# One long convolution's taps on TensorE, and an output projection that begins with the other half

## The chip, the cores and the metric

The kernel runs as one program on one core of a Trainium2 chip. The metric is the device time of one execution in microseconds (us). The core has five engines with a queue each, which run in order and wait for each other by semaphores: TensorE (PE, with its weight loads as PEld), VectorE (DVE), ScalarE (ACT), GpSimd (POOL) and SyncE (SP, which here only starts transfers).

## The reference

It is one step of a two-layer model on 128 context and 512 latent tokens (640 columns here), all in float32. Layer 0 mixes tokens by two convolutions, layer 1 by attention; each is followed by a SwiGLU feed-forward block (FFN). The change touches layer 0's mixer only:

```
u = h @ w_in
ya = gate_b * depthwise_conv(gate_c * xa, sc_w)            # short: 3 taps, 512 channels
z = ub[..., :512] * sigmoid(ub[..., 512:])
z = depthwise_conv(z, cf_dw_w) + cf_dw_b                   # long: 31 taps, 512 channels
z = silu(layernorm(z, cf_ln_g, cf_ln_b))                   # over the 512 channels
return concatenate([ya, z], axis=-1) @ w_out + b_out
```

Context and latent tokens are convolved as separate sequences. What follows needs the mixer's whole output row: an RMS norm, the residual sum, a second RMS norm, and then the FFN.

## The kernel before

Activations lie with channels on the 128 partitions and tokens in the free dimension. A long-convolution channel block is a tile `z0` to `z3`, a short one a tile `m0` to `m3`. Tokens are worked in two chunks: GA, columns 0 to 255, and GB, columns 256 to 639. A dense product is made from three reduced products (`mm3`, lines 175, 187 and 189: high by high, high weight by low input, low weight by high input); the weight's high part is an ACT cast (`whi`, line 134), its low part a subtraction on DVE or POOL (`wlo`, line 139). PE passes of these products are named by their output: `ub`, `gc`, `xa`, `gb` for the input projection, `po` for the output projection, `pg` and `pu` for the first FFN products.

`conv` computes the long convolutions' input first (`ub`), and then, while PE computes `gc`, `xa` and `gb`, DVE runs the 31 taps of each z tile as multiply-adds (line 798): tiles 0 and 1 over all tokens at once (`acl`, 670 columns with pads), tiles 2 and 3 in two groups, the first enough for GA, the second for GB (`acd`). `conv_norm` is the layer norm of one chunk: column sums on PE (`lnm`, `lnv`), the mean and the reciprocal root spread back to all partitions by PE (`spread`), the rest on DVE and ACT. `conv_out` splits the normed z into high and low, and for each chunk multiplies z and m by `w_out`: 64 mm3 steps of 3 passes for GA, and 64 for GB. `boundary` turns a chunk's output into the FFN's input `h` (two sums of squares `st`, two `spread`s, and work on DVE, ACT and POOL); GA's runs while PE does GB's output projection, GB's while PE does the FFN's first products for GA.

The order of instructions on each engine is fixed when the program is built. The taps and the norms are generators in the list `fine`; every mm3 step of a projection advances them by a tick (`lin`), at the low priority TAP_PRIO, and a scheduler then places every instruction in its engine's queue by priority and by its own idea of when inputs are ready. TAP_STEPS = 2 lets two DVE taps go per tick; TAP_ORDER is the order of tiles and groups.

Of the kernel before, what the change touches and what calls it, by code (L numbers as in the profile page):

```python
# [12 lines left out]
AF = mybir.ActivationFunctionType  # L13
ALU = mybir.AluOpType
# [3 lines left out]
P = 128  # L18
D = 1024
KD = D // P  # L20
SEQ = 128
LAT = 512
# [6 lines left out]
CFK = 31  # L29
# [8 lines left out]
AB = ((0, 256), (256, 384))  # L38
# [12 lines left out]
TAP_PRIO = -500  # L51
TAP_STEPS = 2

TAP_ORDER = ((0, None), (1, None), (2, 0), (3, 0), (2, 1), (3, 1))
XCOPY = ('dve',) * 8
SQ_DVE = (1,) * 8
ADD_DVE = (3, 6)
# [17 lines left out]
class Net:  # L75
# [688 lines left out]
    def conv(self, H, M, ada):  # L764
# [20 lines left out]
        def taps(src, wcol, K, pad, bias, out, per, group=None):  # L785
# [21 lines left out]
            c = max(a, st)  # L807
            tap(t, out[:, SEQ + c - st:SEQ + b - st], src[:, t + c:t + b], acc[:, c - a:n])

        zs = [self.ty(f"z{j}") for j in range(4)]  # L810
        made, normed = set(), set()
        for z in zs:
            zero_pads(z, 15)
        self.mix("dve")
# [2 lines left out]
        for hb, chs in ((0, GA), (0, GB), (1, AB)):  # L817
            b2 = self.block(w, 0, KD, 3 * SCW + 512 + 256 * hb, 256)
            b1 = self.block(w, 0, KD, 3 * SCW + 256 * hb, 256)
            sgs = []  # L820
            for i in range(2):
                j = 2 * hb + i
                p2 = self.lin(b2, i * P, P, H, chs, "ub2")
                sgs.append(self.t5([P, TOK], name="sgm"))
                for c, (s, n) in enumerate(chs):
                    nc.scalar.activation(sgs[i][:, s:s + n], p2[c][:, :n], AF.Sigmoid, bias=cb[:, 4 + j:5 + j])
            for i in range(2):
                j = 2 * hb + i
                z = zs[j]
                p1 = self.lin(b1, i * P, P, H, chs, "ub1")  # L830
                sg = sgs[i]
                for c, (s, n) in enumerate(chs):
                    dst, src, g = padded(z, 15, p1[c][:, :n], sg[:, s:s + n], s)
                    nc.vector.scalar_tensor_tensor(dst, src, cb[:, j:j + 1], g, ALU.add, ALU.mult)
                if chs != GA:
                    made.add(j)
            if hb == 0 and chs == GB:
                long = lambda j, per, g: taps(zs[j], lambda t: cw[:, 4 * t + j:4 * t + j + 1], CFK, 15,
                                              par["conv_cf_dw_b"][:, j:j + 1], zs[j], per, g)
                def stream(*todo):  # L840
                    todo = list(todo)
                    while todo:
                        at = next((i for i, (j, _) in enumerate(todo) if j in made), None)
                        if at is None:
                            yield
                            continue
                        j, g = todo.pop(at)
                        yield from long(j, 1, g)
                        for x in ((0, 1) if g is None else (g,)):
                            seen[x] += 1  # L850
                            if seen[x] == 4:
                                yield from self.conv_norm(zs, (GA, GB)[x])
                                normed.add(x)
                seen = [0, 0]
                self.fine.append(self.rate(stream(*TAP_ORDER), TAP_STEPS))
        scw = par["conv_sc_w"]
        for hb in range(2):
            bc = self.block(w, 0, KD, SCW + 256 * hb, 256)
# [20 lines left out]
            for i in range(2):  # L879
# [5 lines left out]
                m = self.t5([P, 2, TOK], R32, name=f"m{j}")  # L885
                self.split((m[:, 0], m[:, 1]), ya[:, :TOK])
                M.append(m)
        while 0 not in normed:
            with self.tc.high_priority(TAP_PRIO):
                self.tick(self.fine)  # L890
        return zs

    def conv_norm(self, zc, ch):

# [35 lines left out]
    def conv_out(self, w, M, Z, zs, Y, bias, after, between):  # L930

        nc = self.nc
        self.mix("pool", "dve")
        gens = []
        for ch in (GA, GB):
            if ch == GB:
                for g in self.fine + self.bg:
# [5 lines left out]
            Yg = Y(ch)  # L943
            for cb in range(4):
                wt = self.block(w, 4, 4, cb * 256, 256) + self.block(w, 0, 4, cb * 256, 256)
                for i in range(2):
                    o = 2 * cb + i
                    ps = self.lin(wt, i * P, P, Z + M, ch, "po")
                    nc.scalar.activation(Yg[o], ps[0][:, :n], AF.Identity, bias=bias[:, o:o + 1])
            gens.append(self.spawn_b(after(Yg, ch)))  # L950
        self.finish(gens[0])
        return gens[1]
# [527 lines left out]
    def run(self):  # L1480
# [13 lines left out]
        zs = self.conv(H, M, self.ada_whole(0, range(4, 10)))  # L1494
        Z = [self.t5([P, 2, TOK], R32, name=f"z{j}") for j in range(4)]
        box = {}

# [9 lines left out]

        def rows(ch):

            (s, n), = ch  # L1510
            if ch == GA:
                first = self.t5([P, 4, n], name="yoa")
                box["rest"] = [self.ty(f"yo{k}") for k in range(4, KD)]
                return [first[:, k] for k in range(4)] + [t[:, s:s + n] for t in box["rest"]]
            return [self.ty(f"yo{k}")[:, s:s + n] for k in range(4)] + [t[:, s:s + n] for t in box["rest"]]

        late = self.conv_out(I["conv_w_out"][0], M, Z, zs, rows, self.par["conv_b_out"], after, between)
        box2 = {}
        ada1 = self.ada_steps(((0, 10, 2), (1, 0, 4), (1, 4, 6)))

# [109 lines left out]
```

## Time and profile before

| | before |
|---|---|
| time of 3 runs, us | median 1736.71 (1735.44 to 1738.82) |
| the profiled execution | 1737.27 us, its span 1735.5 us |
| PE busy | 1635.7 us, 94% of the span |
| DVE busy | 1115.9 us, 64% |
| ACT busy | 669.3 us, 39% |
| chain that ended last | PE 76%, DVE 17% of the span |

Times inside the profile are microseconds from the span's start. Matmuls overlap, so what a pass costs is read from one start to the next, not from its duration (a 256-column pass lasts 0.28 and the next starts 0.12 later). An F32 product is shown as two passes. In a merged line "x2" is the count of passes, and the bracket at a line's end is the idle time ahead of it and what ended it. The mixer's last `po` pass ends, and the FFN's first product starts, at 341.20.

### The profile page before, as it was taken

The page shows a single profiled execution, that of the slowest core. Times are in us where ns is not written, and L with a number is a line of the kernel's source. Part 1 is how long each engine was busy: PE and PEld are TensorE (multiplying, and loading weights), DVE is VectorE, ACT ScalarE, POOL GpSimd, SP SyncE. Part 2 cuts the span into 40 slices and gives each one's busy share as a digit, 9 for nine tenths or more (in the row PEclk, how much of TensorE's full clock was granted, in tenths as well). Part 3 has the DMA queues.
Part 4 walks back from the last instruction along what each step waited for, and adds up shares of the span by engine and source line. Part 5 has one row for each costly group of instructions (what it writes and reads, how often), then busy time and mean ns, then how long its engine had stood idle before and what let it go on. Part 6 is the DMA issues. An engine that isn't in the chain of part 4 may idle for free.

```text
span 1735.5 us, 26938 instructions
## 1 busy us (share of the span) xinstructions
PE 1635.7 (94%) x10549; PEld 1533.4 (88%) x10549; DVE 1115.9 (64%) x2134; ACT 669.3 (39%) x1287; POOL 394.0 (23%) x319
## 2 busy tenths in 40 slices
PE   7999967989999999999898899989998999999998
PEld 3587767989999999999787798779998999999998
DVE  6389997789774725987989755775999102111236
ACT  4321125543232212235444576774642222212234
POOL 1000012443000000002534221124433243333323
PEclk9999988989999999999989999999999999999999
DMA  9543423246463423555433000025355232222233
GB/s 344 160 126 116 129 71 113 77 134 199 154 194 110 150 82 115 183 160 169 126 107 78 13 25 25 1 66 174 107 170 164 61 98 73 73 74 73 73 100 108
DMA packets 183408, 198.65 MB, mean 114 GB/s; under 512 B 21651, under 2 KB 155744, under 8 KB 183280
## 3 DMA queue, kind: packets, MB, share of 16 engines
q1 hardware_dynamic: 181232, 195.34, 36.3%
q8 instruction: 83, 1.36, 0.3%
q10 hardware_dynamic: 1600, 1.48, 0.3%
q14 instruction: 45, 0.37, 0.1%
q0 software_dynamic: 448, 0.11, 0.0%
HBM read 191.37 MB, written 5.52 MB: 113 GB/s over the span
## 4 chain that ended last, share of the span: by engine, by line
PE 76%; DVE 17%; issue 3%; ACT 2%; DMA 1%; POOL 0%; SPq 0%; DVEq 0%; ACTq 0%; POOLq 0%
PE pd L175 5%; PE pd L187 5%; PE pd L189 5%; PE pu L175 5%; PE pu L187 5%; PE pu L189 5%; PE pg L187 5%; PE pg L189 5%; PE pg L175 5%; PE av L1417 3%; PE adaw L491 3%; DVE sq L548 2%; PE pT L973 2%; PE po L175 2%; PE po L189 2%
## 5 line engine op out<-in xcount | busy, mean ns | idle before, releaser
L134 ACT CAST whi<-raw 128x1024 fp32r<-128x1024 f32 (+1 forms) x260 | 263.2, 1017 | 439.2 <-PE pd L187 112.3
L139 POOL TENSOR_TENSOR wlo<-raw,whi 128x1024 fp32r<-128x1024 f32 (+3 forms) x120 | 284.1, 2371 | 555.0 <-ACT whi L134 520.1
L139 DVE TENSOR_TENSOR wlo<-raw,whi 128x1024 fp32r<-128x1024 f32 (+3 forms) x148 | 186.1, 1258 | 107.3 <-ACT whi L134 106.6
L655 DVE TENSOR_TENSOR sg<-pu,sg 128x320 f32<-128x320 f32 (+2 forms) x88 | 39.9, 483 | 247.5 <-PE pu L189 247.5
L189 PE MATMUL pd<-hid,wlo 128*128 128x320 f32 (+2 forms) x704 | 181.5, 310 | 0.0
L175 PE MATMUL pd<-hid,whi 128*128 128x320 f32 (+2 forms) x704 | 181.5, 310 | 0.0
L187 PE MATMUL pd<-hid,whi 128*128 128x320 f32 (+2 forms) x704 | 181.4, 309 | 0.0
L175 PE MATMUL pg<-h,whi 128*128 128x320 f32 (+2 forms) x704 | 177.3, 312 | 3.3 <-DVE sg L655 3.3
L175 PE MATMUL pu<-h,whi 128*128 128x320 f32 (+2 forms) x704 | 178.8, 313 | 0.0
L187 PE MATMUL pu<-h,whi 128*128 128x320 f32 (+2 forms) x704 | 178.4, 313 | 0.0
L189 PE MATMUL pu<-h,wlo 128*128 128x320 f32 (+2 forms) x704 | 178.0, 312 | 0.0
L187 PE MATMUL pg<-h,whi 128*128 128x320 f32 (+2 forms) x704 | 177.8, 312 | 0.0
L189 PE MATMUL pg<-h,wlo 128*128 128x320 f32 (+2 forms) x704 | 177.2, 311 | 0.0
L386 DVE SCALAR_TENSOR_TENSOR acc<-adaw,cT,acc 128x512 f32<-128x512 f32 x196 | 159.4, 865 | 5.6 <-DMA adaw<-in_ada_w 4.9
L175 PEld LDWEIGHTS pg<-h,whi 128*128 128x128 f32 x704 | 123.2, 190 | 3.6 <-DVE sg L655 3.6
L175 PEld LDWEIGHTS pu<-h,whi 128*128 128x128 f32 x704 | 124.6, 192 | 0.0
L187 PEld LDWEIGHTS pu<-h,whi 128*128 128x128 f32 x704 | 124.6, 192 | 0.0
L189 PEld LDWEIGHTS pu<-h,wlo 128*128 128x128 f32 x704 | 124.5, 192 | 0.0
L187 PEld LDWEIGHTS pg<-h,whi 128*128 128x128 f32 x704 | 123.3, 190 | 0.4 <-DVE h L540 0.2
L189 PEld LDWEIGHTS pd<-hid,wlo 128*128 128x128 f32 x704 | 123.6, 189 | 0.0
L187 PEld LDWEIGHTS pd<-hid,whi 128*128 128x128 f32 x704 | 123.5, 189 | 0.0
L175 PEld LDWEIGHTS pd<-hid,whi 128*128 128x128 f32 x704 | 123.5, 189 | 0.0
(473 smaller groups left out, 3354.8 us busy)
## 6 DMA issues: line engine op xcount, KB each, us to landing
adaw<-in_ada_w SPq DMA_DIRECT2D x112, 256.0 KB, 3.0
raw<-in_ffn_w_gate SPq DMA_DIRECT2D x56, 512.0 KB, 3.7
raw<-in_ffn_w_up SPq DMA_DIRECT2D x56, 512.0 KB, 3.7
raw<-in_ffn_w_down SPq DMA_DIRECT2D x56, 512.0 KB, 3.5
raw<-in_conv_w_in SPq DMA_DIRECT2D x24, 512.0 KB, 4.5
raw<-in_ada_w SPq DMA_DIRECT2D x24, 512.0 KB, 4.2
ada0w<-in_ada_w SPq DMA_DIRECT2D x16, 512.0 KB, 10.7
raw<-in_conv_w_out SPq DMA_DIRECT2D x16, 512.0 KB, 3.6
```

The source lines that it names most:

```text
L134: nc.scalar.copy(hi[:, :kt, :cols], rv)
L139: (self.nc.vector if (le or next(self.lo_mix)) == "dve" else self.nc.gpsimd).tensor_tensor(o, x, h, ALU.subtract)
L175: ins = [mm(o, whi, h, start=first, stop=False) for o, (h, l) in zip(outs, xs)]
L187: mm(o, whi, l, start=False, stop=False)
L189: mm(o, wlo, h, start=False, stop=last)
L386: ins = nc.vector.scalar_tensor_tensor(acc[v], w, self.cT[:, v, k:k + 1], acc[v], ALU.mult, ALU.add)
L491: nc.tensor.matmul(ps[:2, :], self.cM[:, k0 + k], w[:, k], start=(k0 + k == 0), stop=(k0 + k == KD - 1))
L548: src = (nc.vector if SQ_DVE[k] else nc.gpsimd).tensor_tensor(q, q, acc, ALU.add)
L655: nc.vector.tensor_tensor(tv(sg[i]), uv, tv(sg[i]), ALU.mult)
L973: self.nc.tensor.transpose(ps, src, self.ident[:m, :m])
L1417: nc.tensor.matmul(av[:, :u.w], value(h, k), pt_[:, 0, i] if u.qt == 0 else pt_[:, :, i], start=(i == 0 and q_ == 0), stop=(i == len(ks) - ...
```

## The change

Tile 1's taps leave DVE. For each of the 31 taps ACT scales the identity matrix by that tap's column of coefficients (`dg`, a 128x128 diagonal in F32), and PE multiplies the shifted z tile by it in F32, once over GA's 256 columns and once over GB's 384, summing all taps in two PSUM tiles (`tap`). Two ACT passes add the bias and write z1 back. Every chunk's layer norm now waits for tile 1 (`tapped`). The generator gives a tap every third tick (TAP_PE_STEPS = 3).

The output projection starts with the m half for GA (all 8 output blocks) and for GB's blocks 4 to 7; ACT writes these sums with the bias. Only then the program waits for GA's norm. Then comes the z half for GA, added by DVE to what lies there; for GB, blocks 0 to 3 are made as before from z and m together, and blocks 4 to 7 from z alone, added by DVE. The PE passes of the projection are as many as before; the weight blocks it loads are 14 instead of 16.

```diff
-TAP_ORDER = ((0, None), (1, None), (2, 0), (3, 0), (2, 1), (3, 1))
+TAP_ORDER = ((0, None), (2, 0), (3, 0), (2, 1), (3, 1))
+TAP_PE = 1
+TAP_PE_STEPS = 3
...
+        def matrix_taps(j):
+            st = SEQ + 30
+            while j not in made:
+                yield
+            ps = [self.sp("tap")[:, :n] for _, n in AB]
+            ps[0] = ps[0].rearrange("p (s n) -> p s n", s=2)
+            for t in range(CFK):
+                d = t2("dg", P, 4)
+                nc.scalar.mul(d, self.ident, cw[:, 4 * t + j:4 * t + j + 1])
+                for o, x in zip(ps, (zs[j][:, t:t + 2 * st].rearrange("p (s n) -> p s n", s=2)[:, :, :SEQ],
+                                     zs[j][:, t + st + SEQ:t + st + LAT])):
+                    nc.tensor.matmul(o, d, x, start=(t == 0), stop=(t == CFK - 1))
+                yield
+            for o, (s, n) in zip(ps, AB):
+                x = zs[j][:, s:s + n]
+                nc.scalar.activation(x.rearrange("p (s n) -> p s n", s=2) if s == 0 else x, o, AF.Identity,
+                                     bias=par["conv_cf_dw_b"][:, j:j + 1])
+            tapped.add(j)
...
-                            if seen[x] == 4:
+                            if seen[x] == 3:
+                                while TAP_PE not in tapped:
+                                    yield
                                 yield from self.conv_norm(zs, (GA, GB)[x])
...
-                self.fine.append(self.rate(stream(*TAP_ORDER), TAP_STEPS))
+                self.fine += [self.rate(stream(*TAP_ORDER), TAP_STEPS), self.rate(matrix_taps(TAP_PE), 1 / TAP_PE_STEPS)]
...
+        def half(cb, k0, X, ch, outs, add):
+            wt = self.block(w, k0, 4, cb * 256, 256)
+            if len(X) > 4:
+                wt += self.block(w, 0, 4, cb * 256, 256)
+            for i in range(2):
+                o = 2 * cb + i
+                ps = self.lin(wt, i * P, P, X, ch, "po")
+                for p, (_, n), y in zip(ps, ch, outs):
+                    if add:
+                        nc.vector.tensor_tensor(y[o], p[:, :n], y[o], ALU.add)
+                    else:
+                        nc.scalar.activation(y[o], p[:, :n], AF.Identity, bias=bias[:, o:o + 1])
+        for cb in range(4):
+            half(cb, 0, M, AB if cb > 1 else GA, [Yg, rest], False)
+        while 0 not in normed:
+            with self.tc.high_priority(TAP_PRIO):
+                self.tick(self.fine)
...
             for cb in range(4):
-                wt = self.block(w, 4, 4, cb * 256, 256) + self.block(w, 0, 4, cb * 256, 256)
-                for i in range(2):
-                    o = 2 * cb + i
-                    ps = self.lin(wt, i * P, P, Z + M, ch, "po")
-                    nc.scalar.activation(Yg[o], ps[0][:, :n], AF.Identity, bias=bias[:, o:o + 1])
+                if ch == GB and cb < 2:
+                    half(cb, 4, Z + M, ch, [Yg], False)
+                else:
+                    half(cb, 4, Z, ch, [Yg], True)
```

In the built order PE meets the 31 taps late: 19 of them before the last `gb` pass, 8 among the `po` passes of the m half, and 4 behind all of these. The 62 products stand in 48 groups between other passes. The first place is PE's queue from the end of the input projection to GA's norm. Before, the norm's sums follow the last `gb` pass at once, and the whole output projection follows the norm:

```order
L187 MATMUL gb<-h_410,whi 128x256
L187 MATMUL gb<-h_410,whi 128x384
L189 MATMUL gb<-h_410,wlo 128x256
L189 MATMUL gb<-h_410,wlo 128x384
L306 MATMUL lnm<-con,lna 128x1 x2
L313 MATMUL spread<-con,mun 128x128 x2
L306 MATMUL lnv<-con,lnq 128x1 x2
L313 MATMUL spread<-con,rzn 128x128 x2
L306 MATMUL lnm<-con,lna 128x1 x3
L313 MATMUL spread<-con,mun 128x128 x3
L175 MATMUL po<-z_2234,whi 128x256 x4
```

Now (from the last pass of the m half on; `m_2326` is m3):

```order
L192 MATMUL po<-m_2326,wlo 128x384
L825 MATMUL tap<-z_498,dg 128x256
L825 MATMUL tap<-z_498,dg 128x384
L825 MATMUL tap<-z_498,dg 128x256
L825 MATMUL tap<-z_498,dg 128x384
L825 MATMUL tap<-z_498,dg 128x256
L825 MATMUL tap<-z_498,dg 128x384
L825 MATMUL tap<-z_498,dg 128x256
L825 MATMUL tap<-z_498,dg 128x384
L309 MATMUL lnm<-con,lna 128x1 x2
L316 MATMUL spread<-con,mun 128x128 x2
L309 MATMUL lnv<-con,lnq 128x1 x2
```

The m half stands ahead of the last taps, and between the last tap and GA's z half PE has only the norm's own small products. The second place is DVE's queue in GA's norm. Before, the ops of the reciprocal root stand between taps of tiles 2 and 3 for GB:

```order
L291 TENSOR_TENSOR rtn<-rgn 128x2
L798 SCALAR_TENSOR_TENSOR acd<-z_499,pcols_168,acd 128x384
L798 SCALAR_TENSOR_TENSOR acd<-z_500,pcols_168,acd 128x384
L292 TENSOR_TENSOR rtn<-rtn,rhn 128x2
L798 SCALAR_TENSOR_TENSOR acd<-z_499,pcols_168,acd 128x384
L798 SCALAR_TENSOR_TENSOR acd<-z_500,pcols_168,acd 128x384
L294 SCALAR_TENSOR_TENSOR rzn<-rtn,rgn 128x2
L798 SCALAR_TENSOR_TENSOR z_499<-z_499,pcols_168,acd 128x384
```

Now:

```order
L288 TENSOR_SCALAR rgn<-rvn 128x2
L291 TENSOR_SCALAR rhn<-rvn 128x2
L294 TENSOR_TENSOR rtn<-rgn 128x2
L295 TENSOR_TENSOR rtn<-rtn,rhn 128x2
L297 SCALAR_TENSOR_TENSOR rzn<-rtn,rgn 128x2
L294 TENSOR_TENSOR rtn<-rzn 128x2
L295 TENSOR_TENSOR rtn<-rtn,rhn 128x2
```

All taps on DVE stand far ahead of the norm. The third place is PE's queue at the end of the output projection, where GA's `h` becomes ready (`h_2518` and `h_2685` are its first tile). Before, 47 `po` passes stand between the last `spread` of GA's boundary and the FFN:

```order
L189 MATMUL po<-m_2171,wlo 128x384
L175 MATMUL po<-m_2231,whi 128x384
L187 MATMUL po<-m_2231,whi 128x384
L189 MATMUL po<-m_2231,wlo 128x384
L175 MATMUL po<-z_2234,whi 128x384
L313 MATMUL spread<-con,rzb 128x128 x2
L187 MATMUL po<-z_2234,whi 128x384
L189 MATMUL po<-z_2234,wlo 128x384
```

Now none do:

```order
L178 MATMUL po<-z_2332,whi 128x384
L190 MATMUL po<-z_2332,whi 128x384
L192 MATMUL po<-z_2332,wlo 128x384
L316 MATMUL spread<-con,rzb 128x128 x2
L178 MATMUL pg<-h_2685,whi 128x256 x2
L554 MATMUL st<-con,sq 128x1 x3
L178 MATMUL pu<-h_2685,whi 128x256
```

GB's output projection is 144 passes instead of 192 and all of them stand ahead of that `spread`. From the FFN's first blocks on, the order on every engine is the same as before.

## Rows read from the trace of the kernel before

**Rows 1.** Stretches: span; PE, PEld, DVE, ACT, POOL busy; PE clock; DMA.

```profile
80.00:243.00 163.00, 163.00 (x924) 129.87 (x923) 140.54 (x232) 29.80 (x40) 4.27 (x8) 1.00 0.39 120
243.00:273.00 30.00, 7.87 (x39) 7.38 (x38) 27.83 (x66) 7.54 (x15) 1.21 (x2) 0.56 0.19 62
273.00:300.00 27.00, 24.64 (x203) 24.45 (x202) 17.80 (x36) 18.17 (x32) 9.59 (x4) 0.98 0.38 118
300.00:343.00 43.00, 40.73 (x224) 40.13 (x225) 34.76 (x95) 25.86 (x54) 13.94 (x10) 0.92 0.32 99
343.00:381.00 38.00, 31.24 (x224) 30.80 (x223) 30.45 (x57) 14.69 (x25) 21.79 (x11) 0.87 0.36 111
```

**Rows 2.** Timeline of PE, end of input projection to output projection: start, length.

```profile
243.63 0.46 PE L189 MATMUL gb<-h,wlo 128*128 128x256 f32 x2
243.93 0.50 PE L306 MATMUL lnm<-con,lna 128*128 128x1 f32 x4
248.16 1.22 PE L313 MATMUL spread<-con,mun 128*128 128x128 f32 x4 [3.73 <-DVE mun L907]
257.68 0.99 PE L306 MATMUL lnv<-con,lnq 128*128 128x1 f32 x4 [8.30 <-DVE lnq L918]
268.26 1.19 PE L313 MATMUL spread<-con,rzn 128*128 128x128 f32 x4 [9.59 <-DVE rzn L294]
...
272.33 0.56 PE L175 MATMUL po<-z,whi 128*128 128x256 f32 x1
```

**Rows 3.** Tile acl: the taps of tiles 0 and 1 on DVE.

```profile
L798 DVE SCALAR_TENSOR_TENSOR acl<-z,pcols,acl x58: 905/916/921, 93.2 to 210.4; 128x670 f32<-128x670 f32 x58
```

**Rows 4.** Timeline of PE, F32 products among reduced ones.

```profile
221.02 0.38 PE L175 MATMUL xa<-h,whi 128*128 128x256 f32 x1
221.34 1.02 PE L491 MATMUL adaw<-raw,cM 128*2 128x512 f32 x2
222.29 0.44 PE L175 MATMUL xa<-h,whi 128*128 128x384 f32 x1
...
986.09 2.33 PE L1417 MATMUL av<-ptw,Vg 128*128 128x256 f32 x10
...
988.39 0.31 PE L1351 MATMUL s<-kL,qS 128*128 128x320 f32 x1
```

**Rows 5.** Timeline of DVE, ops of the layer norms.

```profile
251.48 1.41 DVE L912 TENSOR_TENSOR z<-spread,z 128x256 f32<-128x256 f32 x4
...
288.29 0.15 DVE L285 TENSOR_SCALAR rgn<-rvn 128x3 int32<-128x3 int32 x1
...
290.54 0.16 DVE L294 SCALAR_TENSOR_TENSOR rzn<-rtn,rzn 128x3 f32<-128x3 f32 x1
```

**Rows 6.** Timeline of PE, GA's last output pass to GB's boundary.

```profile
296.58 0.28 PE L187 MATMUL po<-m,whi 128*128 128x256 f32 x1
296.70 0.28 PE L189 MATMUL po<-m,wlo 128*128 128x256 f32 x1
...
301.24 0.94 PE L551 MATMUL st<-con,sq 128*128 128x1 f32 x4 [0.29 <-DVE sq L548]
...
309.98 0.61 PE L313 MATMUL spread<-con,rzb 128*128 128x128 f32 x4
...
310.60 0.34 PE L189 MATMUL po<-m,wlo 128*128 128x384 f32 x1
...
332.48 0.71 PE L313 MATMUL spread<-con,rzb 128*128 128x128 f32 x4 [1.64 <-DVE rzb L294]
...
341.20 0.40 PE L175 MATMUL pg<-h,whi 128*128 128x256 f32 x2
...
351.62 0.94 PE L313 MATMUL spread<-con,rzb 128*128 128x128 f32 x6 [3.36 <-DVE rzb L294]
...
370.02 1.41 PE L551 MATMUL st<-con,sq 128*128 128x1 f32 x6 [3.40 <-DVE sq L548]
```

**Rows 7.** Timeline of DVE, low parts of the second half of GA's h.

```profile
341.16 2.19 DVE L540 SCALAR_TENSOR_TENSOR h<-yo,mods,h 128x128 fp32r<-128x128 f32 x8
```

More of the change, by code (lines that the diff above doesn't have):

```diff
@@ L808, in taps @@
             tap(t, out[:, SEQ + c - st:SEQ + b - st], src[:, t + c:t + b], acc[:, c - a:n])
+        def matrix_taps(j):
[16 more added lines that the diff above has]
+            tapped.add(j)
         zs = [self.ty(f"z{j}") for j in range(4)]
-        made, normed = set(), set()
+        made, normed, tapped = set(), set(), set()
         for z in zs:
@@ L887, in conv @@
                 M.append(m)
[L888 to L891, printed above, removed]
+        return zs, normed
     def conv_norm(self, zc, ch):
@@ L928, in conv_norm, with conv_out @@
                                  bias=par["conv_cf_ln_b"][:, j:j + 1])
-    def conv_out(self, w, M, Z, zs, Y, bias, after, between):
+    def conv_out(self, w, M, Z, zs, normed, Y, bias, after, between):
         nc = self.nc
@@ L934, in conv_out @@
         gens = []
+        Yg = Y(GA)
+        rest = Y(None)
+        def half(cb, k0, X, ch, outs, add):
[15 more added lines that the diff above has]
+                self.tick(self.fine)
         for ch in (GA, GB):
@@ L942, in conv_out @@
                 self.split((Z[j][:, 0, s:s + n], Z[j][:, 1, s:s + n]), zs[j][:, s:s + n])
-            Yg = Y(ch)
+            if ch == GB:
+                Yg = Y(GB)
             for cb in range(4):
-                wt = self.block(w, 4, 4, cb * 256, 256) + self.block(w, 0, 4, cb * 256, 256)
-                for i in range(2):
-                    o = 2 * cb + i
-                    ps = self.lin(wt, i * P, P, Z + M, ch, "po")
-                    nc.scalar.activation(Yg[o], ps[0][:, :n], AF.Identity, bias=bias[:, o:o + 1])
+                if ch == GB and cb < 2:
+                    half(cb, 4, Z + M, ch, [Yg], False)
+                else:
+                    half(cb, 4, Z, ch, [Yg], True)
             gens.append(self.spawn_b(after(Yg, ch)))
@@ L1493, in run @@
         M = []
-        zs = self.conv(H, M, self.ada_whole(0, range(4, 10)))
+        zs, normed = self.conv(H, M, self.ada_whole(0, range(4, 10)))
         Z = [self.t5([P, 2, TOK], R32, name=f"z{j}") for j in range(4)]
@@ L1508, in rows @@
         def rows(ch):
-            (s, n), = ch
             if ch == GA:
-                first = self.t5([P, 4, n], name="yoa")
+                first = self.t5([P, 4, GA[0][1]], name="yoa")
                 box["rest"] = [self.ty(f"yo{k}") for k in range(4, KD)]
-                return [first[:, k] for k in range(4)] + [t[:, s:s + n] for t in box["rest"]]
-            return [self.ty(f"yo{k}")[:, s:s + n] for k in range(4)] + [t[:, s:s + n] for t in box["rest"]]
-        late = self.conv_out(I["conv_w_out"][0], M, Z, zs, rows, self.par["conv_b_out"], after, between)
+                return [first[:, k] for k in range(4)] + [t[:, :GA[0][1]] for t in box["rest"]]
+            (s, n), = GB
+            rest = [t[:, s:s + n] for t in box["rest"]]
+            return ([None] * 4 if ch is None else [self.ty(f"yo{k}")[:, s:s + n] for k in range(4)]) + rest
+        late = self.conv_out(I["conv_w_out"][0], M, Z, zs, normed, rows, self.par["conv_b_out"], after, between)
         box2 = {}
```

## The prediction, made before the changed kernel ran

> **What bounds the kernel now.** I read the busy times by stretch first. From 80 to 243 us, where the input projection runs, PE is busy 163.00 of 163 us at full clock, and DVE, which does the taps beside it, 140.5 [rows 1]. So the mixer up to the last `gb` pass is bound by PE, and what is added to PE there is added to the time. From 243 on it is different: PE is busy 7.9 of 30 us, then 24.6 of 27, 40.7 of 43 and 31.2 of 38, and from its clock (0.56, 0.98, 0.92, 0.87) one sees that it falls to its lower level in the gaps [rows 1]. PE's idle time there is 22.1 + 2.4 + 2.3 + 6.8 = 33.6 us, and that is nearly all there is to win.
>
> The timeline of PE says what the first gap is: GA's layer norm. After the last `gb` pass (243.93) PE waits 3.73, 8.30 and 9.59 us for the norm's small steps, and the output projection starts at 272.33 [rows 2]. Each step waits on DVE, which is busy 27.8 of the 30 us [rows 1] with taps for GB that stand between the norm's ops in its queue. After that, GA's output projection runs to 296.81, GA's boundary takes until the `spread` at 332.48, and the FFN starts at 341.20 [rows 6]. The last 6.8 us idle are two waits of 3.36 and 3.40 us in GB's boundary [rows 6].
>
> **What the change takes away and adds.** From DVE it takes one of the two `acl` tiles: half of 58 multiply-adds of 0.914 us, 26.5 us [rows 3], and a few short ones. DVE was not the bound before 243; after it, the norm no longer finds taps in its way.
>
> To PE it adds 62 F32 products. The trace has their like: ten F32 passes of 256 columns with 128x128 F32 weights start at 986.09, and the second pass behind them starts at 988.39; less 0.13 for the 320-column pass between, a pass costs 0.217 us, and a product is two passes [rows 4]. So 256 columns cost 0.433 and, by columns, 384 cost 0.65: 1.083 per tap, 33.6 us for 31. For going from reduced products to F32 and back the rows give two ends. Around the `adaw` product (two columns of weights, two passes of 512) the one pass between two such groups takes 0.32 instead of 0.12 (the way back from one and into the next), and the product 0.95 instead of 0.87; together about 0.30 per group [rows 4]. Around the F32 `spread` (128 columns of weights, four passes of 128, 0.43 by the price above) everything from 309.98 to 310.60 is 0.62, of which 0.18 is the reduced pass between: 0.01 extra [rows 6]. The taps' weights have 128 columns like the `spread`'s, so I take 0.05 for each of the 48 groups, 2.4 us. A tap is then 1.16 us, all of them 36 us (33.6 to 48 by the two ends). None of it lies beside other work: PE has no idle time up to 243, and by its new order it has none in the m half.
>
> On weights there is a rule that speaks against the change. The Trainium skill ("TensorE: Matmul & The Clock Gate", section "Weight-path perf modes") says that the fast weight load is not used for FP32 weights, and its section "LDWEIGHTS" gives a load columns / 1.2 in ns, an estimate of 107 ns here. With two loads for each of 62 products, that would be 13 us more if no load hid behind a product; the 0.217 per F32 pass above shows no load between passes, so the trace does not bear that out where F32 passes follow each other.
>
> ACT gets 31 small scalings and two passes over the taps. It is busy 29.8 of 163 us [rows 1], and the first four diagonals are made long before they are used, so I cost them at nothing. If a diagonal came late behind a weight cast in ACT's queue, each time would cost PE up to one cast, and 31 of these would be far out of the range; the order has each diagonal ahead of its product by one to four, so I keep nothing for it.
>
> Now the path, step by step, in the time of the profiled trace.
> - End of `gb`: 243.9 + 19 taps x 1.16 = 266.0.
> - The m half: 96 passes of 256 columns at 0.12 [rows 6] and 48 of 384 at 0.18 (a `gb` pair of both is 0.30 [rows 2]), 20.1 us, with 12 taps, 13.9: 300.0. This is work moved, not added, but it does not fill the wait for the norm: in the new order it stands ahead of the last four taps, and the norm needs all 31.
> - GA's norm, now alone. From the end of the last tap for GA (0.65 before that of GB's): the ACT pass with the bias about 0.5, three adds of 0.35 (a fourth of 1.41 [rows 5]), `lnm` 0.50, `spread` 1.22, four subtractions 1.41, squares and their adds 0.9 (from the same op sizes), `lnv` 0.99, the reciprocal root 2.4 (288.29 to 290.70 [rows 5]), and 4.07 from the second `spread` to the first `po` pass [rows 2]; with nine handovers of some 0.15 (half of the 0.29 in [rows 6], an estimate) 14.4 us. The bounds are the ops alone, 11, and the 24.2 that lie between 248.16 and 272.33 before. PE is idle for most of it. The z half starts at 300.0 - 0.65 + 14.4 = 313.8.
> - GA's z half: 96 passes x 0.12 = 11.5, and 1.5 at the lower clock, as before (272.33 to 296.81 is 24.5 for 192 passes worth 23.0): 326.8. Before it was 296.8, so GA's output is 30 us later, though nothing of it was waiting on taps of GA before.
> - GA's boundary: 35.7 us from there to the `spread` at 332.48 [rows 6]. It is a chain through DVE, ACT and POOL and stays. PE's 144 passes for GB (26 us) fit into it, so the 48 passes that GB no longer needs are saved where PE waits anyway. I take off 2 us, since the last squares come sooner and the weights' low parts are fewer: `spread` at 360.5, 28 later.
> - The FFN's start: before, PE had `po` passes to do for 8.7 us behind that `spread`, and the last part of h came at 343.35, 10.9 behind it [rows 6, 7]. Now PE has none, and waits for h; the first 48 `pg` passes (5.8 us) can't end before h is there, as if the FFN started 5.2 behind the `spread`, at 365.7: 24.5 later than 341.2.
> - GB's boundary: its chain goes on behind GA's h on DVE, now with fewer squares before it (about 3 us), so it is 28 - 3 = 25 later, and the two waits of 3.4 stay. From there on the order is the same, PE is bound again, and nothing gives it back.
>
> The sum is +25 us on the profiled execution's own 1737.27 (span 1735.5 and 1.8 around it), 1762.3. The median of the runs is 0.6 lower than the profiled execution, so I predict 1762. In PE's terms: 36 us of products are added, and of 33.6 us of idle time only some 11 go, since the norm of 14 and the wait for h take the place of the others.
>
> **Rivals.**
> - *Not slower: the F32 taps cost what reduced passes cost.* 0.12 + 0.18 per tap instead of 1.16 takes off 27 us: -2, 1735. The point from which the change is no loss is 0.35 us per tap ((36 - 25) / 31). For it: no row shows a 384-column F32 pass. Against it: the five `av` products and the `adaw` product of [rows 4], each two passes, and each pass 1.7 to 1.8 times as long as a reduced one of as many columns.
> - *Every group pays the way in and out.* 48 x 0.30 instead of 0.05, all on PE's bound stretch: +12, 1774. For it: the `adaw` rows, and the page's rule on F32 weights points the same way. Against it: the `spread` among `po` passes.
> - *The boundaries shrink.* With DVE free of 26 us, GB's chain gets ahead of the FFN and the two waits (6.8) go; and GA's boundary, 35.7 us, gets a sixth shorter on a DVE with less to do, 6 us: -13, 1749. For it: DVE is busy 34.8 of 43 and 30.5 of 38 us there [rows 1]. Against it: none of the removed taps stands behind 268 us, so that load is not theirs.
> - *The change doesn't do what it says* holds in part and is in the sum: the m half fills the wait for taps, not for the norm.
>
> **How the numbers follow.** The forecast has 0.66; its own range is 1753 to 1771 (tap price 1.083 to 1.25, norm 11 to 17, boundary 0 to 4 off). Groups that pay: 0.13. Boundaries that shrink: 0.14. Taps as cheap as reduced passes: 0.07, which I split in 0.03 faster and 0.04 within 0.2%, since that case lies at -2 us. A difference of 0.2% (3.5 us) is about what a measurement tells from none. The first three cases are all slower by more than that: 0.93. The range takes in the whole of the forecast and most of the two beside it, 1748 to 1775.
>
> **What would show it.** Right: `tap` passes of 256 columns some 0.22 from start to start, no PE idle up to the last tap, the last tap near 300; then a gap of 12 to 15 us at the lower clock to the first z pass near 314; a second gap ahead of the first `pg`, which starts some 20 to 25 us later than 341. DVE's last tap well ahead of the last `gb` pass. Wrong: if the last tap is over by 285, the price of a product is off; if GA's z half starts less than 8 us behind it, the chain of the norm is; if `pg` starts within 10 us of 341 though the last tap is at 300, PE's order in the boundary mattered more than the chain; and if the FFN's start is 25 later but the end is not, something behind it had slack that [rows 1] do not show.

## The result and the profile after

The changed kernel takes 1768.7 us (median of 4 runs, 1767.5 to 1770.0) against 1736.1 for the kernel before beside it: ratio 1.0177, 95% interval 1.0164 to 1.0190, 32.6 us slower. The profiled execution's span is 1767.0 us, 31.5 more than that of before. The forecast was 1762, so the sign and the range (1748 to 1775) held, and the added time was forecast 7 us too short.

By stretch, the profile after reads so (from:to in us, length, busy time of PE, PEld, DVE, ACT and POOL with counts, PE's granted clock, DMA share, GB/s):

```profile
80.00:266.00 186.00, 186.00 (x1022) 147.08 (x1021) 131.49 (x232) 39.64 (x62) 5.11 (x8) 1.00 0.34 105
266.00:300.00 34.00, 30.30 (x176) 26.23 (x174) 5.74 (x12) 14.43 (x30) 4.80 (x3) 0.99 0.31 99
300.00:330.00 30.00, 21.45 (x132) 20.81 (x132) 24.43 (x66) 14.20 (x27) 4.97 (x2) 0.73 0.19 59
330.00:373.00 43.00, 34.47 (x177) 33.70 (x178) 35.36 (x97) 22.61 (x49) 13.58 (x9) 0.82 0.24 71
373.00:412.00 39.00, 31.68 (x237) 31.50 (x237) 29.54 (x62) 16.22 (x27) 17.27 (x10) 0.85 0.36 109
```

PE is full up to the last tap, which ends at 295, and so for 51 us longer than in [rows 1]. DVE, 27.8 of 30 us busy in GA's norm before, is now busy for 5.7 of the 34 us up to 300. From 266 on PE still idles 3.7 + 8.6 + 8.5 + 7.3 = 28 us, of the 33.6 of before: the change added PE work and kept most of the gaps.

The same on PE's timeline (start, duration, operation, in brackets the idle time before it and what ended it):

```profile
293.81 1.24 PE L825 MATMUL tap<-z,dg 128*128 128x256 f32 x4
296.31 0.58 PE L309 MATMUL lnm<-con,lna 128*128 128x1 f32 x4 [1.27 <-DVE lna L925]
...
301.18 0.99 PE L309 MATMUL lnv<-con,lnq 128*128 128x1 f32 x4 [3.27 <-DVE lnq L940]
304.48 1.19 PE L316 MATMUL spread<-con,rzn 128*128 128x128 f32 x4 [2.31 <-DVE rzn L297]
...
308.55 1.20 PE L178 MATMUL po<-z,whi 128*128 128x256 f32 x4
...
322.56 0.28 PE L192 MATMUL po<-z,wlo 128*128 128x256 f32 x1
326.79 1.62 PE L316 MATMUL spread<-con,rzn 128*128 128x128 f32 x6 [3.96 <-DVE rzn L297]
...
361.70 0.71 PE L316 MATMUL spread<-con,rzb 128*128 128x128 f32 x4 [1.99 <-DVE rzb L297]
365.39 0.79 PE L178 MATMUL pg<-h,whi 128*128 128x256 f32 x2 [2.98 <-ACT h L542]
368.94 1.41 PE L554 MATMUL st<-con,sq 128*128 128x1 f32 x6 [2.76 <-DVE sq L551]
...
398.69 1.41 PE L554 MATMUL st<-con,sq 128*128 128x1 f32 x6 [7.33 <-DVE sq L551]
...
407.28 0.83 PE L316 MATMUL spread<-con,rzb 128*128 128x128 f32 x6
```

GA's norm took 28.4 us from `lnm` to the first `po` pass before [rows 2] and takes 12.2 now, but nothing runs beside it. GA's output ends at 322.7 (296.8 before), yet GB's norm is not ready: PE waits 3.96 us for `rzn`, where it came in time before:

```profile
296.81 0.83 PE L313 MATMUL spread<-con,rzn 128*128 128x128 f32 x6
```

Of the two waits in GB's boundary, the one of 3.36 for `rzb` in [rows 6] is gone, and a new one of 2.76 for squares has come; the other, 3.40 there, is 7.33.

### The profile page after: what moved, and what is told of

It is laid out like the page before. It is cut to its first block, busy times and chain, and to the rows that moved or that the text cites. A ratio compares the mean times of both kernels' runs of the same rounds, so it can differ in the third digit from the quotient of the medians.

```text
span 1767.0 us, 27200 instructions
## 1 busy us (share of the span) xinstructions
PE 1673.1 (95%) x10673; PEld 1561.0 (88%) x10673; DVE 1088.1 (62%) x2113; ACT 680.5 (39%) x1318; POOL 389.2 (22%) x318
## 4 chain that ended last, share of the span: by engine, by line
PE 78%; DVE 15%; issue 3%; ACT 2%; DMA 1%; POOL 1%; SPq 0%; DVEq 0%; ACTq 0%; POOLq 0%
PE pd L178 5%; PE pd L190 5%; PE pd L192 5%; PE pg L190 5%; PE pu L178 5%; PE pg L192 5%; PE pg L178 5%; PE pu L190 5%; PE pu L192 5%; PE av L1461 3%; PE adaw L494 2%; PE tap L825 2%; DVE sq L551 2%; PE s L1397 2%; PE pT L1017 2%
## 5 line engine op out<-in xcount | busy, mean ns | idle before, releaser
L142 POOL TENSOR_TENSOR wlo<-raw,whi 128x1024 fp32r<-128x1024 f32 (+3 forms) x119 | 278.2, 2341 | 594.4 <-ACT whi L137 475.8
L142 DVE TENSOR_TENSOR wlo<-raw,whi 128x1024 fp32r<-128x1024 f32 (+1 forms) x147 | 185.2, 1261 | 128.4 <-ACT whi L137 127.3
L192 PEld LDWEIGHTS pg<-h,wlo 128*128 128x128 f32 x704 | 124.9, 192 | 0.0
L190 PEld LDWEIGHTS pd<-hid,whi 128*128 128x128 f32 x704 | 123.5, 188 | 0.0
```

Of the source, the lines that this page charges most:

```text
L142: (self.nc.vector if (le or next(self.lo_mix)) == "dve" else self.nc.gpsimd).tensor_tensor(o, x, h, ALU.subtract)
L190: mm(o, whi, l, start=False, stop=False)
L192: mm(o, wlo, h, start=False, stop=last)
```

## The experiments

Six points of PE's timeline place every run (us from the span's start; GB's last `spread` is the one behind the last wait above). The last columns are the median and its ratio to before with the 95% interval.

| kernel | `lnm` GA | first z pass | GA output ends | GA's last `spread` | GB's last `spread` | median | ratio |
|---|---|---|---|---|---|---|---|
| before | 243.9 | 272.3 | 296.8 | 332.5 | 378.6 | | |
| after | 296.3 | 308.6 | 322.7 | 361.7 | 407.3 | 1768.7 | 1.0177 |
| order only | 246.5 | 280.0 | 294.0 | 332.8 | 377.0 | 1738.1 | 1.0002 [0.9990, 1.0014] |
| taps only | 277.8 | 290.1 | 315.1 | 349.2 | 394.5 | 1756.2 | 1.0108 [1.0093, 1.0123] |
| taps early | 276.8 | 303.3 | 316.3 | 354.7 | 398.3 | 1762.1 | 1.0140 [1.0124, 1.0155] |
| m half for GA only | 288.9 | 301.6 | 314.7 | 350.8 | 395.8 | 1758.6 | 1.0119 [1.0102, 1.0136] |
| no taps of tile 1 | 243.7 | 257.9 | 282.5 | 316.7 | 362.4 | 1723.7 | 0.9923 [0.9905, 0.9941] |
| no taps, new order | 243.0 | 265.8 | 278.0 | 313.9 | 361.6 | 1723.5 | 0.9912 [0.9896, 0.9929] |
| every second tap | 279.5 | 292.2 | 305.1 | 343.4 | 388.5 | 1747.8 | 1.0065 [1.0050, 1.0079] |
| taps early, GA only | 277.5 | 298.2 | 311.4 | 347.5 | 392.5 | 1756.5 | 1.0114 [1.0100, 1.0128] |

The rows come from several sets of runs, in which the median of before lay between 1736.1 and 1738.8; differences of a few us are safer by the ratios (0.001 is 1.7 us). The points count from the span's start, and part of a difference is there before the first tap. Where the `ub` passes end, the changed kernel is already 2.7 us ahead of before (first line before, second after):

```profile
132.47 0.46 PE L189 MATMUL ub<-h,wlo 128*128 128x256 f32 x2
```

```profile
129.78 0.46 PE L192 MATMUL ub<-h,wlo 128*128 128x256 f32 x2
```

The taps only, the m half for GA only and every second tap are 1.4 to 1.7 us ahead there, the kernels with no taps of tile 1 and a second profile of before within 0.5 us. Why is not known.

### The order alone, and the taps alone

```diff
-TAP_ORDER = ((0, None), (2, 0), (3, 0), (2, 1), (3, 1))
+TAP_ORDER = ((0, None), (1, None), (2, 0), (3, 0), (2, 1), (3, 1))
...
-                self.fine += [self.rate(stream(*TAP_ORDER), TAP_STEPS), self.rate(matrix_taps(TAP_PE), 1 / TAP_PE_STEPS)]
+                self.fine.append(self.rate(stream(*TAP_ORDER), TAP_STEPS))
```

> The change's second part alone: all taps on VectorE as before, the short convolutions' half of the projection ahead of GA's norm. Theory (the products are what costs; the order as such gains): GA's norm takes the 28 us it took before (VectorE still has GB's taps), but 144 output passes run inside it; the z half then takes 13 us in place of the 24.5 us of all 192 passes, so GA's output ends 11 us earlier. GB's norm ends on VectorE where it did, so GB's products start only 3 us earlier behind a wait of 8 us, and the feed-forward 5 to 11 us earlier. Time 1728 us (1723 to 1733). Rival A (the order itself is part of the cost, since GB's norm and the boundary lose their cover): 1736 us or more. Rival B (boundary chains do not move at all): 1734 to 1737 us.

Measured: 1738.06, no change. The theory's 1728 does not hold. The time can't tell the rivals apart (by the ratio, 1736.4 for a before of 1736.1, which both take in), and the trace has something of each: GA's last `spread` stays where it was (332.8 and 332.5), and GB's norm lost its cover. The m half does run inside the norm, but the norm got longer (33.5 us from `lnm` to the first z pass in place of 28.4), since DVE is full with GB's taps (busy 30.00 of 30 us from 243), and GB's norm on DVE ends where it did:

```profile
275.89 1.20 PE L316 MATMUL spread<-con,rzn 128*128 128x128 f32 x4 [7.70 <-DVE rzn L297]
...
297.86 1.62 PE L316 MATMUL spread<-con,rzn 128*128 128x128 f32 x6 [3.70 <-DVE rzn L297]
```

The second line stood at 296.81 without a wait before: PE's earlier end turned into a wait.

The other half of the change, with the old projection (all twelve k blocks behind GA's norm):

```diff
-        for cb in range(4):
-            half(cb, 0, M, AB if cb > 1 else GA, [Yg, rest], False)
...
-                if ch == GB and cb < 2:
-                    half(cb, 4, Z + M, ch, [Yg], False)
-                else:
-                    half(cb, 4, Z, ch, [Yg], True)
+                wt = self.block(w, 4, 4, cb * 256, 256) + self.block(w, 0, 4, cb * 256, 256)
...
+                    ps = self.lin(wt, i * P, P, Z + M, ch, "po")
```

> The change's first part alone: tile 1's taps as F32 products on TensorE, the projection in the order of before (all 12 k blocks of GA behind its norm). Theory: the products add 34 us on TensorE, last tap at 278 us; GA's norm, with VectorE free, takes 13.5 us alone instead of 28.3, so GA's output ends 19 us later than before, and GB's norm has the old 24.5 us of output passes as cover, so all later points are 19 us later too. Time 1756 us (1751 to 1760), under the changed kernel by 10 to 15 us: in the changed kernel GB's 48 short passes (6 us) stand ahead of GA's output and GB's norm has half the cover (4.6 us). Rival (the order gains what it hides, so without it the products cost more): 1769 us or more.

Measured: 1756.17, as forecast, 12.5 below the changed kernel (12.0 by the ratios). `lnm` is 33.9 us later than before, about the price of the 31 taps on a PE that is full (PE was 1.4 ahead when the `ub` passes ended, and 1.3 us are a wait for `lna` that before did not have); the norm is 12.3, and GB's norm has GA's whole output as cover:

```profile
277.83 0.58 PE L309 MATMUL lnm<-con,lna 128*128 128x1 f32 x4 [1.32 <-DVE lna L925]
...
290.13 1.20 PE L178 MATMUL po<-z,whi 128*128 128x256 f32 x4
...
315.10 0.83 PE L316 MATMUL spread<-con,rzn 128*128 128x128 f32 x6
```

### What DVE's relief and the products are worth

Without tile 1's taps on either engine, in both orders. The generator of the products is left out, and the norms wait only for tile 1's input:

```diff
-                self.fine += [self.rate(stream(*TAP_ORDER), TAP_STEPS), self.rate(matrix_taps(TAP_PE), 1 / TAP_PE_STEPS)]
+                self.fine += [self.rate(stream(*TAP_ORDER), TAP_STEPS)]
```

> Leaves out tile 1's taps altogether (neither VectorE nor TensorE computes them; the norm reads the untapped tile); the projection in the order of before. It gives what VectorE's relief is worth without the price of the products. Theory: GA's norm takes 13.5 us with VectorE free in place of 28.3, all else as before, so 15 us are gained: 1722 us (1717 to 1728), and the products cost, by the difference to the products with this order (1756), 34 us, which is 31 times 1.09 us. Rival (relief is worth little, since another chain ends last): 1733 us or more, and the products then cost 23 us or less.

> Leaves out tile 1's taps (as the run without taps), with the changed kernel's order of the projection. It asks where the order costs the 12.5 us that separate the changed kernel (1769) from the products alone (1756), when the order with VectorE taps cost nothing. Theory (the order costs because the short half stands ahead of the last products and of GA's norm without covering it): without products in the queue the short half covers the norm, GA's output ends 7 us earlier than without taps in the old order, the boundary is 4 us longer, so 1721 us (1717 to 1726) against 1723.7. Rival (the order costs by GB's norm and the boundary wherever VectorE is relieved): 1732 us or more.

Measured: 1723.68 and 1723.54. The relief alone is worth 13 us, all of it in GA's norm (28.4 to 14.2 us). The products then cost 1756.2 - 1723.7 = 32.5 us, the theory's 34 within the runs' scatter. Of the second forecast the direction holds (GA's output 4.5 us earlier where 7 were forecast, 2.8 left at GA's last `spread` and 0.8 at GB's); the gain of 3 us does not show. The six medians make the point:

| tile 1's taps | old order | new order |
|---|---|---|
| on VectorE | 1737 (before) | 1738.1 |
| left out | 1723.7 | 1723.5 |
| on TensorE | 1756.2 | 1768.7 |

The order costs nothing by itself, and 12.5 us beside the products. That is not GB's norm, which PE waits 5.26 us for in the new order without taps as well:

```profile
279.62 0.80 PE L309 MATMUL lnv<-con,lnq 128*128 128x1 f32 x6 [1.44 <-DVE lnq L940]
285.67 0.77 PE L316 MATMUL spread<-con,rzn 128*128 128x128 f32 x2 [5.26 <-DVE rzn L297]
```

Here the m half covers the norm; in the changed kernel it stands ahead of the last four taps, so the norm begins 18.5 us later than with the taps alone (296.3 against 277.8) and runs uncovered.

The slope was taken by every second tap, spaced as before in the issue order. One thing moves with it: the last tap now comes 24 `po` passes ahead of `lnm`, so part of the norm's head is covered.

```diff
-            for t in range(CFK):
+            for t in range(0, CFK, 2):
...
+                if t < CFK - 1:
+                    yield
```

> The changed kernel with every second tap of tile 1 left out (16 of 31 products, as far apart in the issue order as the 31 were). Theory (a price of 1.09 us per tap, 1:1 on the end): 15 times 1.09 = 16.4 us under the changed kernel, 1752 us (1750 to 1755). Rival (much of the price is fixed: the order, the eviction, a switch between kinds of product per group): less than 10 us under it, 1759 us or more.

Measured: 1747.77, 20.9 below the changed kernel (19.5 by the ratios), more than forecast. At `lnm` the 15 taps are worth 16.9 us, 1.12 each, so the rival with a fixed price is out; 1.9 more come up to GB's last `spread` and the rest behind it. The 16.9 hold two small things that nearly cancel: the changed kernel was 1.1 us further ahead before any tap, and its `lnm` waits 1.27 us where this one's has no wait.

### What the m half does ahead of the last taps

Only GA's part of it (96 passes in place of 144):

```diff
-            half(cb, 0, M, AB if cb > 1 else GA, [Yg, rest], False)
+            half(cb, 0, M, GA, [Yg, rest], False)
...
-                if ch == GB and cb < 2:
+                if ch == GB:
```

> The changed kernel, but only GA's short half goes ahead of its norm (96 passes in place of 144); GB's output is made whole, 192 passes, behind GB's norm. Theory: 48 passes less ahead of the last tap bring GA's output 6 us forward and GB's 48 passes 6 us longer; the feed-forward waits for GA's chain on VectorE and ScalarE more than for GB's passes, so it starts 0 to 6 us earlier. Time 1765 us (1761 to 1769). Rival (GB's passes end last in the boundary): 1769 us or more.

Measured: 1758.58, 10 below the changed kernel, below the range I gave. GA's output comes 8.0 us earlier: the 48 passes have 384 columns and cost 8.6 us at 0.18, not the 6 of the forecast. And GB's 48 passes more cost nothing: GA's last `spread` is 10.9 earlier and GB's 11.5. So the change had moved those passes from where PE waits to where GA's norm waits for PE. The boundary (GA's output to GA's last `spread`) takes 36.1 in place of 39.0.

The products at high priority, so that all stand ahead of the last gate pass:

```diff
+                with self.tc.high_priority(900):
                     d = t2("dg", P, 4)
                     nc.scalar.mul(d, self.ident, cw[:, 4 * t + j:4 * t + j + 1])
...
                         nc.tensor.matmul(o, d, x, start=(t == 0), stop=(t == CFK - 1))
```

> The changed kernel, but with the diagonal products issued at high priority, so that the last stands ahead of the gate products' end and none among the output passes. Same products, same bytes. Theory: TensorE is through with the gates at 278 us, GA's norm (13.5 us) then runs inside the 18.5 us of the short half, the z half ends at 309.5 us in place of 322.7; GB's norm is done 30.5 us behind the first norm product as in the changed kernel, at 311, so GB's products start 16 us earlier. Time 1755 us (1750 to 1759). Rival (what bounds is TensorE's total work in the stage, the late taps cost nothing): 1768 us.

Measured: 1762.14, 6.5 below the changed kernel, between the two forecasts. `lnm` is where I put it, but the norm takes 26.4 us:

```profile
280.87 0.60 PE L316 MATMUL spread<-con,mun 128*128 128x128 f32 x4
...
295.38 0.50 PE L309 MATMUL lnv<-con,lnq 128*128 128x1 f32 x4
299.21 1.19 PE L316 MATMUL spread<-con,rzn 128*128 128x128 f32 x4 [3.33 <-DVE rzn L297]
```

`lnv` starts without a wait: DVE had its sums ready at 287.0, and it stood behind 96 passes of the m half in PE's queue. Cover put into a queue in order holds up the chain that it is to cover. That was tested with both edits together, which leave 48 passes between the two steps:

> Products early (as in the run with the early taps) and only GA's short half ahead of its norm. Theory: lnv's product stands behind 48 output passes in place of 96 in TensorE's queue, so GA's norm and its output come 6 us earlier than with the early taps alone (1762), and GB's boundary is the 36 us of the run with GA's half alone in place of 38: 1753 us (1750 to 1757). Rival (VectorE's norm is late in any case): 1757 us or more, no better than GA's half alone.

```profile
281.51 0.60 PE L316 MATMUL spread<-con,mun 128*128 128x128 f32 x4
...
289.95 0.80 PE L309 MATMUL lnv<-con,lnq 128*128 128x1 f32 x4 [2.09 <-DVE lnq L941]
```

Measured: 1756.45. `lnv` comes 5.4 earlier and now waits for DVE, as expected, and the time is in the forecast's range, at its upper end; from the rival (1757 or more) and from GA's half alone the intervals don't tell it apart.

### Three attempts to beat both

Since PE idled 22 us in GA's norm, products of another tile were put there: tile 1 back on DVE, GB's part of tile 3 on PE (`while seen[0] < 4: yield` holds its generator until GA's norm starts).

```diff
+            o = self.sp("tap")[:, :n]
...
+                nc.tensor.matmul(o, d, zs[j][:, a + t:a + t + n], start=(t == 0), stop=(t == CFK - 1))
```

> Another place for the products: all of tile 1 back on VectorE, and GB's part of tile 3 (31 products of 384 columns, about 0.65 us each by the two passes of 128x384 in the trace, 20 us) on TensorE while GA's norm runs, where TensorE idled 22 of 30 us; 24 of them are queued between the norm's products, 7 among the first output passes. The projection in the order of before. Theory (products cost nothing in idle time, and VectorE ends last there): VectorE loses 14 us of taps that lay inside GA's norm, so the norm ends 4 to 12 us earlier, less 4.5 us for the 7 late products; GB's norm starts later than in the kernel before. 1732 us (1726 to 1738). Rival (the products hold the norm's own matmuls up in the queue, and GB's norm is exposed): 1740 us or more.

Then, without products, GA's norm was issued at a higher priority, with the old and (both norms) the new order:

```diff
+        with self.tc.high_priority(2000 if ch == GA else 0):
             a, b = t2("lna"), t2("lnb")
...
```

With the new order it reads `high_priority(2000)`.

> No products: all taps on VectorE and the projection in the order of before. GA's norm alone is issued at a higher priority than what stands around it: its first product now stands among the products before the gates, its variance inside the gates, and its instructions on VectorE ahead of GB's taps. It asks whether VectorE's relief can be had by order alone. Theory: GA's norm took 28 us because 40 of GB's taps stand between its instructions, and began only behind the gates; begun earlier, it ends by 250 to 256 us in place of 272, GA's output at 280 in place of 297; VectorE's total stays, so GB's norm ends 5 to 10 us earlier at most and sets GB's start. 1730 us (1724 to 1736). Rival (VectorE's total work bounds up to GB's norm, so only the idle time moves behind GA's output): 1736 us or more.

> No products: all taps on VectorE; both norms issued at the higher priority, and the changed kernel's order of the projection (the short half of 144 passes ahead of GA's norm). Theory: the short half fills the time in which GA's norm ends, GA's output ends at 275 us in place of 297; GB's norm ends 10 to 15 us earlier than before and sets GB's start, with 48 passes less behind it. 1725 us (1718 to 1732). Rival (as with the order alone, the time between GA's output and the feed-forward is a chain on VectorE that takes what was gained): 1734 us or more.

Measured: 1739.90, ratio 1.0018 [1.0006, 1.0030]; 1740.83, 1.0021 [1.0011, 1.0030]; 1738.54, 1.0009 [1.0000, 1.0017]. None is faster than before, and none of the three theories holds. The first z pass did come earlier, by 7.6 us at 264.8 and by 9.9 at 262.4 in the first two (in the third it came at 272.9). Both then lost it to GB's norm, in the first of them so:

```profile
293.67 0.72 PE L309 MATMUL lnv<-con,lnq 128*128 128x1 f32 x6
301.74 0.76 PE L316 MATMUL spread<-con,rzn 128*128 128x128 f32 x2 [7.34 <-DVE rzn L297]
```

In the second, GA's norm began at 222.4, 21 us earlier, and PE idled all the same, since its small ops on DVE stand between GB's taps:

```profile
258.53 1.22 PE L316 MATMUL spread<-con,rzn 128*128 128x128 f32 x4 [15.13 <-DVE rzn L297]
```

What held GB's norm up in these two is not DVE's work alone. In the second, DVE has the sum of GB's tiles (`lna`) ready at 268.40, as before (268.64), but PE takes the last of its `lnm` products behind GA's output passes, some 19 us later than before. DVE first, then PE:

```profile
267.84 0.56 DVE L924 TENSOR_TENSOR lna<-lna,lnb 128x384 f32<-128x384 f32 x1
```

```profile
288.15 0.28 PE L192 MATMUL po<-m,wlo 128*128 128x256 f32 x1
288.27 0.50 PE L309 MATMUL lnm<-con,lna 128*128 128x1 f32 x4
```

Before, all of them stood ahead of GA's output:

```profile
269.24 1.28 PE L306 MATMUL lnm<-con,lna 128*128 128x1 f32 x6
```

In the first it is the same, `lna` ready at 275.4 and the last `lnm` at 284.0, with DVE busy only 13.0 of the 30 us from 243; in the third DVE is full there (29.96 of 30). It is again a norm's product behind output passes in a queue. A kernel with GA's norm early and GB's `lnm` ahead of GA's output was not run, so that DVE bounds this stretch whatever the order is not shown. No version that was run beats the kernel before and computes all of it.

### The kernel before once more

> The kernel before once more, for a second profile of it. In all eight kernels so far the first down product moved by 1 to 5 us less than the median of the runs against before. Theory 1 (the first profile of before was fast in layer 1): its first down product is at 469 us again, its end 1 to 4 us later than 1735.5. Theory 2 (the changed kernels lose 2 us in layer 1): span within 1 us of 1735.5.

Measured: first down product 469.6, span 1736.7, so theory 1 holds, near the lower end of its 1 to 4 us. In the changed kernel the first down product is 28.7 us later (497.8), the span 31.5. Of the 2.9 us between these the second profile of before takes 0.7. Most of the rest is lost at the start of layer 1's FFN, where the same stretch, 28.7 us later, runs at a lower granted clock behind the gap (first line before, second after; both profiles of before show 0.91):

```profile
1260.00:1280.00 20.00, 16.58 (x127) 16.41 (x126) 16.85 (x35) 11.39 (x20) 5.91 (x3) 0.91 0.58 180
```

```profile
1288.70:1308.70 20.00, 16.25 (x111) 16.08 (x111) 14.50 (x32) 9.44 (x17) 6.00 (x3) 0.83 0.50 159
```

Why it stays lower there was not settled. The other kernels' profiles lost between 0.5 and 5.5 us behind the first down product.

## Why the prediction was right, and where 7 us were missing

Right were the sign and its reason: the products are added one to one on a PE that is full, and the m half fills the wait for taps and not for the norm. The taps-only and half-taps runs show the first, the table of six the second. By its steps, in profile time:

- *Tap price 1.16, 36 us.* 33.9 us by `lnm` with the taps alone, 1.09 each; 1.12 by the half taps. In the changed kernel the `gb` passes, with 19 taps among them, end 18.2 us later than before (262.1) though the `ub` passes had ended 2.7 earlier: 20.9, 1.10 each. The 0.05 for changing between F32 and reduced products is not there: here two F32 passes of 384 columns and one reduced pass of 0.18 lie between 281.43 and 282.26, 0.83 in all, and 0.65 is the bare price.

```profile
281.31 0.28 PE L192 MATMUL po<-m,wlo 128*128 128x256 f32 x1
281.43 0.81 PE L825 MATMUL tap<-z,dg 128*128 128x384 f32 x2
281.78 0.64 PE L192 MATMUL po<-m,wlo 128*128 128x384 f32 x1
282.26 0.45 PE L178 MATMUL po<-m,whi 128*128 128x256 f32 x2
```

The rule of the Trainium skill ("TensorE: Matmul & The Clock Gate", "Weight-path perf modes") that F32 weights get no fast load adds nothing to the price of [rows 4] that these rows show, though each tap brings a new weight tile. The rival in which every group pays is out, and so is that of taps as cheap as reduced passes.

- *Last tap at 300.0, GA's output at 326.8.* They came at 295.0 and 322.7, five and four microseconds sooner. Of the five, 2.4 are the 0.05 per group that is not there; the other 2.7 are the lead ahead of the first tap, which the forecast had no term for and whose cause is open. From the last tap to the first z pass it took 13.5 us where the steps gave 13.8, and the z half 14.1 in place of 13.0. (The lower bound of that norm, "the ops alone, 11", was summed wrongly: the terms listed add up to 13.0.)
- *GA's boundary 35.7 less 2.* This step failed. It took 39.0, so GA's last `spread` was 29.2 us later and not 28, though GA's output was only 25.9 later. In my step the boundary was one chain that would get shorter; GB's norm was not in it. Before, GB's norm had the 24.5 us of GA's output as cover; with half the passes it is exposed, 3.96 us. Where GB's norm is covered (the taps alone) the boundary is 34.1, near the 33.7 I gave; with the new order for GA it is 36, and with GB's too, 38 to 39, but 35.9 without tile 1's taps, though GB's norm is exposed there by 5.26. So the exposed norm is not all of it. The reciprocal root at the boundary's end takes DVE 5.6 us from `rvb` to the last `rzb`, before 4.2: the adds of GB's blocks 4 to 7 (`yo`), which the change put on DVE, and their squares stand between its steps. With the new order for GA only, and without tile 1's taps, none of these adds stands there.

```profile
358.32 0.15 DVE L295 TENSOR_TENSOR rtb<-rtb,rhb 128x2 f32<-128x2 f32 x1
358.39 0.55 DVE L970 TENSOR_TENSOR yo<-po,yo 128x384 f32<-128x384 f32 x1
358.86 0.15 DVE L297 SCALAR_TENSOR_TENSOR rzb<-rtb,rzb 128x2 f32<-128x2 f32 x1
```

Of the 3.3 us against before, 1.9 lie ahead of that `rvb`, behind the exposed norm, and 1.4 in the root.
- *FFN's start 365.7.* 365.4. That is luck: GA's output came four too soon and the boundary took five too long, and the FFN starts 3.7 behind the `spread` in place of 5.2, with a wait of 2.76 more behind its first products.
- *GB's boundary 25 later, its waits of 3.4 stay.* The second mis-sized term: GB's last `spread` is 28.7 later, and the waits there, 6.8 in all before, are 10.1 (2.76 and 7.33). The last wait is 7.3 in five kernels with GB's m half moved (4.99 in the one without tile 1's taps) and 3.1 to 4.7 in all others. From GA's last `spread` to GB's the kernels of the table take 43.7 to 47.7 us, with 48 passes more or less; so PE's passes don't set it: fewer of them are longer waits. The waits end with DVE's squares, so a chain through DVE is the likely bound; no run tested it.
- *Nothing behind it.* 2.9 us came later, 2 of them around the stretch at the lower clock in layer 1; the cause is open.

So of the 7 us that were missing 3.7 lie in GB's boundary and 2.9 behind it; the errors up to the FFN's start cancel. The rival of shrinking boundaries failed: GA's grew by 3.3 us, and GB's, from GA's last `spread` to GB's, stayed (46.2 before, 45.6 after).

## What to carry over

Moving work from an engine that is not the bound to one that is costs its full length there; what can come back is only the wait that the relief ends (here 13 us for 33), so weigh these two before placing anything. Work that is to cover a wait must stand between the chain's instructions in the queue: ahead of what the chain needs it delays it, and as one block between two steps it delays the second. When the cover of one chain is halved, look for the next chain that had been under it, and let the passes whose omission only lengthens a wait stay where they are.

## What was not expected of the hardware

A DVE op on 2 or 3 columns, 0.15 us as a rule, took 2.0 and 2.2 us when the subtraction for a weight's low part on POOL ran over it; both lay on the chain that PE waited for. First DVE, then POOL, in the kernel after:

```profile
321.62 2.01 DVE L297 SCALAR_TENSOR_TENSOR rzn<-rtn,rgn 128x3 f32<-128x3 f32 x1
...
359.04 2.21 DVE L294 TENSOR_TENSOR rtb<-rzb 128x2 f32<-128x2 f32 x1
```

```profile
321.05 2.57 POOL L142 TENSOR_TENSOR wlo<-raw,whi 128x1024 fp32r<-128x1024 f32 x1 [2.34 <-ACT whi L137]
...
358.88 2.36 POOL L142 TENSOR_TENSOR wlo<-raw,whi 128x1024 fp32r<-128x1024 f32 x1 [4.32 <-ACT whi L137]
```

The DVE ops end when POOL's do (323.63 and 323.62; 361.25 and 361.24). The Trainium skill ("SBUF — State Buffer", section "SBUF: two separate sides") has VectorE and GpSimd lock a shared pair of ports for a whole instruction, for VectorE's ops with two SBUF inputs; these rows agree. But such stalls are not what made GA's boundary longer, since the kernel before has the second of them at the same step (DVE, then POOL):

```profile
329.81 2.23 DVE L291 TENSOR_TENSOR rtb<-rzb 128x2 f32<-128x2 f32 x1
```

```profile
329.63 2.39 POOL L139 TENSOR_TENSOR wlo<-raw,whi 128x1024 fp32r<-128x1024 f32 x1 [3.99 <-ACT whi L134]
```

It has two more in GB's boundary, 1.08 and 2.28 us from 346.60 on. With the taps early, no small op of GB's norm was hit (two squares on DVE were), and its `rzn` came 4.06 us behind GA's output, in the changed kernel 4.12. No run took these subtractions off POOL, so what they cost was not tested.
